# Reordering the small products of two recurrences (RWKV-7 and retention) in a hybrid decoder block

## The chip, the core and the metric

The kernel runs on one core of a Trainium2 chip. The metric is the device time of one execution in microseconds (us), the median over three executions. Comparisons of kernels are made on the same chip, beside executions of the kernel before.

## What is computed

The block takes x (1 x 1024 tokens x 1024 channels, float32) and returns the same shape. Two token mixers work side by side on the normalised tokens, a merge and an output projection follow, then a gated convolutional FFN. Only the two mixers matter here:

```python
# RWKV-7, 8 heads of 64 channels: one state S (64 x 64) per head, token by token
def step(S, inp):
    r_t, k_t, v_t, w_t, kk_t, a_t = inp
    sa = jnp.einsum('bhvk,bhk->bhv', S, -kk_t)
    S = (S * w_t[:, :, None, :]
         + sa[..., None] * (kk_t * a_t)[:, :, None, :]
         + v_t[..., None] * k_t[:, :, None, :])
    y = jnp.einsum('bhvk,bhk->bhv', S, r_t)
    return S, y
...
# retention, 8 heads (64 channels for queries and keys, 128 for values), chunks of 128 tokens
def step(R, inp):
    qc, kc, vc = inp
    s = jnp.einsum('bihd,bjhd->bhij', qc, kc) * decay_mask
    inner = jnp.einsum('bhij,bjhe->bihe', s, vc)
    cross = jnp.einsum('bihd,bhde->bihe', qc * q_decay, R)
    R = R * chunk_decay + jnp.einsum('bjhd,bjhe->bhde', kc * k_decay, vc)
    return R, inner + cross
```

## The kernel before, in words

All matrix work is done on TensorE (PE in the profile). The large projections are float32 products made exact from two parts: each of them is three products of 128 x 128 weights with 512 columns (lines L198 to L200, `mm3`). The small products of the recurrences are plain float32 products; the hardware runs each of them as two passes, so the profile counts two MATMUL records for one `PE.matmul` of the code.

The program goes in stages. First come the projections of the RWKV branch (`rw_tiles`, products `ps_rw`), with two low-rank products per channel tile and token half: `p_lw` (L400, L401) and `p_a` (L404, L405). Of each, the second part uses half of the rows only (64 of 128). Then come the two recurrences, and the other 40 projection tiles (`qk_pair`, `side_tile`, products `ps_side`) are put between their steps. Nothing in the recurrences needs most of these tiles, so they fill TensorE while the recurrence waits for other engines.

The RWKV recurrence is done in 8 blocks of 128 tokens (j), each with two chunks of 64 tokens (c). Per block and chunk:

- `p_G` (L589): products of keys with queries, 8 heads. Even heads lie on partitions 0 to 63 and odd heads on 64 to 127, so each product uses 64 rows of the array; q is the parity. The four even heads go to one PSUM bank and then the four odd heads to another one (tag "B", two banks). VectorE (DVE) evacuates each bank into `Tt` (L592) and `Gm` (L594).
- An inverse of triangular blocks: `Tt` goes through DRAM (`tt_d`, `tb`), DVE substitutes row by row (L611, L613, tiles `xprod` and `xb`), the result goes through DRAM to `XD`, is transposed by DVE to `X` (L624), and feeds products on 32 x 32 pieces of the array (L632, L639, L649, L657).
- `p_W1` (L685, L689; the profile calls the tile p_W): for each pair of heads a product of the queries with the state (128 rows, 64 columns of the array, L685) and then two head products with `Gm` (64 rows, 64 columns, L689). DVE copies the sum (L691), `p_S` follows (L695, 64 x 64), DVE makes `AV`, then `p_N` (L703, the new state; even and odd heads write different halves of the partitions), and `p_Y` (L716, L719; both 128 rows by 64 columns).

Retention is done in 8 blocks of 128 tokens. `first_stage(j)` transposes the values (`p_v`, L773), makes the masked scores `p_s` (L782, 64 rows of the array, four even heads and then four odd ones, again in two banks), and the next state `p_R` (L795). `second_stage(j)` makes the outputs `p_o` in two banks (tags "C" for even heads, "Y" for odd ones): for each head a product with the state (L818, 64 rows) and one with the scores (L819, all 128 rows), the first only for j > 0. Then come the statistics of the heads (L821), the scaling by ScalarE (ACT) from PSUM into `on` (L834), and transposes `p_y` (L840).

The order on each engine is not the order of the code. A planner with its own cost model places the instructions of all engines; the code gives dependences and buffers, and `tc.high_priority` lifts some of them. So a change in the code moves instructions that it does not name.

The core of `p_W1` and `p_o` before:

```python
for i in range(4):
    if not fresh:
        PE.matmul(p_W1[q, i * 128:(i + 1) * 128], AR[:, i, 1 + c, :], state[:, i, :],
                  start=True, stop=False)
    for h in (2 * i, 2 * i + 1):
        hs = slice(64 * h, 64 * h + 64)
        PE.matmul(p_W1[q, hs], Gm[c][o, hx(h), 64 - 64 * c:128 - 64 * c], AV[c][o, hs],
                  start=fresh, stop=fresh or h % 2 == 1)
```

Of the kernel before, what the change touches and what calls it, by code (L numbers as in the profile page):

```python
# [41 lines left out]
def constants():  # L42
# [8 lines left out]
    # columns that sum the even and the odd head of tile i: rows 2i, 2i+1 of 8 (two sums of 8 rows)  # L51
# [12 lines left out]
    # rows 8g..8g+7 of the unit matrix of 16 for the partitions of group g  # L64
# [8 lines left out]
    # decays of the queries (halved: the gate adds the factor), their squares (even heads, then odd), those of the keys  # L73
# [32 lines left out]
def layout(a):  # L106
# [12 lines left out]
    # columns of the rotated queries and keys: first halves of four heads, then their second halves  # L119
# [24 lines left out]
def body(tc, nc, xT, pos, wch, wbrw, wbret, wout, wup, wdn, w2a2, gw2, rows, vecs, consts0, consts1, out):  # L144
    V, S, G, PE = nc.vector, nc.scalar, nc.gpsimd, nc.tensor
    ctx = ExitStack()
    with ctx:
# [23 lines left out]
        def bank(name, tag="A"):  # L171
            return psB.tile([128, 512], F32, tag=tag, name=name, bufs=BANKS[tag])
# [4 lines left out]
        def load_w(src, kt, full=None, hi=None, lo=None, st=None):  # L177
            """Weights [128, kt, 128] as the exact sum of two float32r parts (in st, hi, lo if given)."""
# [33 lines left out]
        def rms_bcast(pool, ss, nt, tags="AA", mem=None, to=None):  # L212
            """ss holds partial sums of squares over channels, for nt tiles of 128 tokens; returns the
            reciprocal root mean square of each token on all partitions, in PSUM
            (or in to, by four tiles)."""
# [36 lines left out]
        with tc.tile_pool(name="x0", bufs=2, reuse_waits="tile") as xp:  # L252
            # the tokens go into the products before their norm, which scales what comes out
# [43 lines left out]
        # ---- RWKV projection with token shift, and what the recurrence needs of each channel tile:  # L297
        # decayed queries, key directions and keys, for all tokens
# [5 lines left out]
        with pctx, tc.tile_pool(name="p1", bufs=1, reuse_waits="tile", side="right") as p1:  # L304
# [12 lines left out]
            def rw_tiles(tiles, ws):  # L317
                """Column tiles of w_in with the token shift; of several, the first two go by quarters of the tokens at first."""
# [43 lines left out]
            # the inputs of the low-rank products as two parts, stacked on the partitions  # L362
# [4 lines left out]
            # the other products take the tokens with their norm  # L367
# [24 lines left out]
            for i in range(4):  # L392
# [4 lines left out]
                for hf in range(2):  # L397
# [3 lines left out]
                    PE.matmul(p_lw, wll[0:64, 0, ch], LW[0:64, h_], start=False, stop=True)  # L401
# [3 lines left out]
                    PE.matmul(p_a, wll[64:128, 1, ch], LA[64:128, h_], start=False, stop=True)  # L405
                    S.activation(ta[:, h_], p_a, AF.Tanh, bias=a0h[:, i1], scale=0.5)
                # decays: their sums from the start of each chunk
# [43 lines left out]
                for c in range(2):  # L451
                    # the chunks of a pair swapped
                    o = 2048 + 128 * i + 64 * (1 - c)
                    nc.scalar.dma_start(L_d[:, :, o:o + 64].rearrange("j p t -> p j t"), v_.rearrange(jct, c=2, t=64)[:, :, c, :])
            # the sums over each head's channels, token-major; those for the values with the chunks swapped
# [12 lines left out]
            # rotary tables, packed: sines, then cosines, each by halves of the tokens  # L468
# [21 lines left out]
        # ---- the other projections: rotated queries and keys, values, gates  # L490
        pj_d = dp.tile([40, 128, T], F32, name="pj_d")

        def qk_pair(m):
            """Tiles 14 + 2m, 15 + 2m of w_in: both halves of the queries or keys of four heads."""
# [26 lines left out]
        def side_tile(i):  # L521
            """Column tile i of w_in (22..29 v, 30..37 g, 38..53 gates)."""
# [15 lines left out]
        # ---- RWKV-7 in chunks of 64 tokens, two chunks (one tile of 128 tokens) at a time  # L538
# [24 lines left out]
        for j in range(NJ):  # L563
# [7 lines left out]
            # token-major values, chunk c in the rows of the other one  # L571
# [8 lines left out]
            # products of the keys with the queries  # L580
            Gm = []
            Tt = r2.tile([128, 8, 64], F32, name="Tt")
            for c in range(2):
                gm = r2.tile([128, 8, 128], F32, tag=f"Gm{c}", name="Gm")
                for q in range(2):
                    p_G = bank("p_G", "B")
                    lo = 64 * q
                    for i in range(4):
# [692 lines left out]
```

## Time and profile before

| what | value |
|---|---|
| runs of the kernel before | 1952.18, 1954.6 and 1958.46 us, median 1954.6 |
| span of the profiled execution | 1949.9 us, the one time of that execution that the page gives |
| PE, PEld (weight loads) | busy 95% and 75% of the span |
| DVE, ACT, POOL | busy 61%, 33% and 38% of the span |
| mean granted TensorE clock | 0.978 |
| chain of work that ended last | PE 60%, DVE 21%, DMA 7%, issue 5%, POOL 4%, ACT 3% |
| RWKV recurrence | about 240 to 746 us of the span |
| retention | about 760 to 918 us |
| last `ps_side` product, first merge product after it | 951.4 and 951.7 us |

The span runs from the first to the last instruction of one execution. A matmul's duration in the profile is a modelled latency, and matmuls are pipelined: what one costs the engine is read from its start to the start of the next one. The shape "64*128" in a row means 64 rows by 128 columns of the array. The granted clock is given as a share of full speed: 1.0 is 2.4 GHz and 0.5 is 1.2 GHz.

### The profile page before, as it was taken

The page shows a single profiled execution, that of the slowest core. Times are in us where ns is not written, and L with a number is a line of the kernel's source. Part 1 is how long each engine was busy: PE and PEld are TensorE (multiplying, and loading weights), DVE is VectorE, ACT ScalarE, POOL GpSimd, SP SyncE. Part 2 cuts the span into 40 slices and gives each one's busy share as a digit, 9 for nine tenths or more (in the row PEclk, how much of TensorE's full clock was granted, in tenths as well). Part 3 has the DMA queues.
Part 4 walks back from the last instruction along what each step waited for, and adds up shares of the span by engine and source line. Part 5 has one row for each costly group of instructions (what it writes and reads, how often), then busy time and mean ns, then how long its engine had stood idle before and what let it go on. Part 6 is the DMA issues. An engine that isn't in the chain of part 4 may idle for free.

```text
span 1949.9 us, 27421 instructions
## 1 busy us (share of the span) xinstructions
PE 1848.0 (95%) x10626; PEld 1471.4 (75%) x10626; DVE 1191.9 (61%) x2003; ACT 650.3 (33%) x999; POOL 742.9 (38%) x534
## 2 busy tenths in 40 slices
PE   6889989999999999999999999789999999999996
PEld 5667877777777778777788878567777777778885
DVE  7885474744565534564253855879988887753413
ACT  4544221111111112232244334444444444543320
POOL 4755433221221022011264753654544544322523
PEclk8899999999999999999999999899999999999998
DMA  4443532342333225444563643533222222675521
GB/s 170 135 135 119 180 92 64 109 111 86 100 99 101 68 71 173 147 140 131 204 201 104 225 145 126 184 122 108 87 76 87 67 76 74 211 216 154 184 89 43
DMA packets 203841, 244.43 MB, mean 125 GB/s; under 512 B 61120, under 2 KB 136384, under 8 KB 202688
## 3 DMA queue, kind: packets, MB, share of 16 engines
q1 hardware_dynamic: 126864, 171.11, 28.3%
q10 hardware_dynamic: 76848, 71.59, 11.3%
q8 instruction: 83, 1.36, 0.3%
q14 instruction: 46, 0.38, 0.1%
HBM read 177.10 MB, written 65.54 MB: 124 GB/s over the span
## 4 chain that ended last, share of the span: by engine, by line
PE 60%; DVE 21%; DMA 7%; issue 5%; POOL 4%; ACT 3%; ACTq 0%; SPq 0%; DVEq 0%; POOLq 0%
PE ps_side L200 7%; PE ps_side L198 7%; PE ps_side L199 7%; DVE u_f L1037 4%; PE ps_dn L200 4%; PE ps_dn L198 3%; PE ps_dn L199 3%; DVE u_f L1039 2%; POOL w_lo L1131 2%; PE ps_rw L198 2%; PE ps_rw L199 2%; PE ps_rw L200 2%; DVE w_sa L1135 2%; PE ps_o L199 1%; PE ps_o L200 1%
## 5 line engine op out<-in xcount | busy, mean ns | idle before, releaser
L192 POOL TENSOR_TENSOR w_lo<-w_st,w_hi 128x1024 fp32r<-128x1024 f32 (+2 forms) x107 | 250.7, 2344 | 508.2 <-PE ps_side L200 174.3
L187 ACT CAST w_hi<-w_st 128x1024 fp32r<-128x1024 f32 (+2 forms) x162 | 161.8, 999 | 441.8 <-PE ps_side L199 160.1
L199 PE MATMUL ps_side<-hnl,w_hi 128*128 128x512 f32 x640 | 255.8, 400 | 0.0
L200 PE MATMUL ps_side<-hnh,w_lo 128*128 128x512 f32 x640 | 255.5, 399 | 0.0
L198 PE MATMUL ps_side<-hnh,w_hi 128*128 128x512 f32 x640 | 255.3, 399 | 0.0
L192 DVE TENSOR_TENSOR w_lo<-w_st,w_hi 128x1024 fp32r<-128x1024 f32 (+1 forms) x55 | 71.8, 1306 | 139.2 <-ACT w_hi L187 42.4
L200 PEld LDWEIGHTS ps_side<-hnh,w_lo 128*128 128x128 f32 x640 | 121.0, 189 | 26.6 <-issue 0.8
L199 PEld LDWEIGHTS ps_side<-hnl,w_hi 128*128 128x128 f32 x640 | 121.1, 189 | 26.1 <-issue 1.3
L198 PEld LDWEIGHTS ps_side<-hnh,w_hi 128*128 128x128 f32 x640 | 120.9, 189 | 25.7 <-issue 0.5
L1037 DVE SCALAR_TENSOR_TENSOR u_f<-ub,vct,u_f 128x512 f32<-128x512 f32 x88 | 103.4, 1179 | 9.5 <-ACT u_f L1036 9.5
L1131 POOL TENSOR_TENSOR w_lo<-w_st,w_hi 128x512 fp32r<-128x512 f32 (+1 forms) x53 | 106.0, 2024 | 1.7 <-issue 1.6
L1036 ACT ACTIVATE u_f<-ub,vct 128x512 f32<-128x512 f32 x76 | 60.0, 813 | 123.6 <-DVE ub L1169 102.3
L199 PE MATMUL ps_rw<-hnl,w_hi 128*128 128x512 f32 (+1 forms) x224 | 89.3, 399 | 9.8 <-DVE hnl L269 8.8
L198 PE MATMUL ps_rw<-hnh,w_hi 128*128 128x512 f32 (+1 forms) x224 | 88.1, 397 | 9.1 <-ACT hnh L268 7.1
L200 PE MATMUL ps_rw<-hnh,w_lo 128*128 128x512 f32 (+1 forms) x208 | 81.0, 390 | 0.0
L200 PE MATMUL ps_b<-y_hi,w_lo 128*128 128x512 f32 x192 | 75.4, 393 | 1.9 <-POOL w_lo L192 1.0
L198 PE MATMUL ps_b<-y_hi,w_hi 128*128 128x512 f32 x192 | 75.4, 393 | 0.4 <-ACT w_hi L187 0.4
L199 PE MATMUL ps_b<-y_lo,w_hi 128*128 128x512 f32 x192 | 75.3, 392 | 0.0
L200 PE MATMUL ps_dn<-f_k,w_lo 128*128 128x512 f32 (+1 forms) x198 | 73.0, 369 | 0.0
L198 PE MATMUL ps_dn<-f_k,w_hi 128*128 128x512 f32 (+1 forms) x198 | 72.9, 368 | 0.0
L1039 DVE SCALAR_TENSOR_TENSOR u_f<-ub,vct,u_f 128x512 f32<-128x512 f32 x88 | 72.7, 843 | 0.2
L199 PE MATMUL ps_dn<-f_k,w_hi 128*128 128x512 f32 (+1 forms) x198 | 72.7, 368 | 0.0
(422 smaller groups left out, 4503.2 us busy)
## 6 DMA issues: line engine op xcount, KB each, us to landing
w_st<-in_wup_dram SPq DMA_DIRECT2D x54, 512.0 KB, 3.5
w_st<-in_wch_dram SPq DMA_DIRECT2D x52, 512.0 KB, 3.7
w_st<-in_wdn_dram SPq DMA_DIRECT2D x38, 512.0 KB, 4.0
pj_d<-ot ACTq DMA_DIRECT2D x64, 256.0 KB, 2.0
zvg<-pj_d SPq DMA_DIRECT2D x8, 1536.0 KB, 8.7
f_d<-u_f ACTq DMA_DIRECT2D x44, 256.0 KB, 2.1
L<-L_d SPq DMA_DIRECT2D x8, 1344.0 KB, 6.1
gt<-pj_d SPq DMA_DIRECT2D x32, 256.0 KB, 4.3
```

The source lines that it names most:

```text
L187: S.copy(hi, st)
L192: eng.tensor_tensor(out=lo, in0=st, in1=hi, op=ALU.subtract)
L198: PE.matmul(ps, wh, xh, start=first and a == 0, stop=False, skip_group_check=skip)
L199: PE.matmul(ps, wh, xl, start=False, stop=False, skip_group_check=skip)
L200: PE.matmul(ps, wl, xh, start=False, stop=last and a == n - 1, skip_group_check=skip)
L1036: S.activation(u, src, AF.Identity, bias=VC("cb")[:, i:i + 1], scale=VC("cw2")[:, i:i + 1])
L1037: V.scalar_tensor_tensor(out=u, in0=ub[:, 1:513], scalar=VC("cw1")[:, i:i + 1], in1=u, op0=ALU.mult, op1=ALU.add)
L1039: V.scalar_tensor_tensor(out=u, in0=ub[:, 0:512], scalar=VC("cw0")[:, i:i + 1], in1=u, op0=ALU.mult, op1=ALU.add)
L1131: eng.tensor_tensor(out=w[1][:, ks, :], in0=src, in1=w[0][:, ks, :], op=ALU.subtract)
L1135: V.tensor_tensor(out=sa[:, rh_, :], in0=st1[:, lh, :], in1=st2[:, lh, :], op=ALU.subtract)
```

## The change

Five groups of products are written in another order or another shape; the sums are the same. Comments were dropped too, which shifts nothing but line numbers (L589 becomes L590, L685 becomes L692, L689 becomes L688, L782 becomes L785, L818 becomes L820, L819 becomes L824).

```diff
                     PE.matmul(p_lw, wlh[:, 0, ch], LW[:, h_], start=True, stop=False)
-                    PE.matmul(p_lw, wll[0:64, 0, ch], LW[0:64, h_], start=False, stop=True)
+                    PE.matmul(p_lw, wll[:, 0, ch], LW[:, h_], start=False, stop=True)
...
-                    PE.matmul(p_a, wll[64:128, 1, ch], LA[64:128, h_], start=False, stop=True)
+                    PE.matmul(p_a, wll[:, 1, ch], LA[:, h_], start=False, stop=True)
...
+                p_Gs = [bank("p_G", "B") for q in range(2)]
+
+                for i in range(4):
+                    for q in range(2):
+                        lo = 64 * q
+                        PE.matmul(p_Gs[q][:, i * 128:(i + 1) * 128], BK[lo:lo + 64, i, 2 * c:2 * c + 2, :],
+                                  AR[lo:lo + 64, i, 2 * c:2 * c + 2, :], start=True, stop=True)
                 for q in range(2):
-                    p_G = bank("p_G", "B")
-                    lo = 64 * q
-                    for i in range(4):
-                        PE.matmul(p_G[:, i * 128:(i + 1) * 128], BK[lo:lo + 64, i, 2 * c:2 * c + 2, :],
-                                  AR[lo:lo + 64, i, 2 * c:2 * c + 2, :], start=True, stop=True)
...
-                for i in range(4):
-                    if not fresh:
+
+                for h in range(8):
+                    hs = slice(64 * h, 64 * h + 64)
+                    PE.matmul(p_W1[q, hs], Gm[c][o, hx(h), 64 - 64 * c:128 - 64 * c], AV[c][o, hs],
+                              start=h == 0, stop=fresh, skip_group_check=True)
+                if not fresh:
+                    for i in range(4):
                         PE.matmul(p_W1[q, i * 128:(i + 1) * 128], AR[:, i, 1 + c, :], state[:, i, :],
-                                  start=True, stop=False)
-                    for h in (2 * i, 2 * i + 1):
-                        hs = slice(64 * h, 64 * h + 64)
-                        PE.matmul(p_W1[q, hs], Gm[c][o, hx(h), 64 - 64 * c:128 - 64 * c], AV[c][o, hs],
-                                  start=fresh, stop=fresh or h % 2 == 1)
+                                  start=False, stop=True, skip_group_check=True)
...
+            p_ss = [bank("p_s", "B") for e in range(2)]
+            for i in range(4):
+                for e in range(2):
+                    lo = 64 * e
+                    PE.matmul(p_ss[e][:, i * 128:(i + 1) * 128], Z[lo:lo + 64, 4 + i, :], Z[lo:lo + 64, i, :],
+                              start=True, stop=True)
             for e in range(2):
-                p_s = bank("p_s", "B")
-                lo = 64 * e
-                for i in range(4):
-                    PE.matmul(p_s[:, i * 128:(i + 1) * 128], Z[lo:lo + 64, 4 + i, :], Z[lo:lo + 64, i, :],
-                              start=True, stop=True)
...
-            p_os = []
+            p_os = [bank("p_o", "CY"[e]) for e in range(2)]
+
+            if j:
+                for i in range(4):
+                    for e in range(2):
+                        lo = 64 * e
+                        PE.matmul(p_os[e][:, i * 128:(i + 1) * 128], Z[lo:lo + 64, i, :], Rj[lo:lo + 64, i, :],
+                                  start=i == 0, stop=False, skip_group_check=True)
             for e in range(2):
-                p_o = bank("p_o", "CY"[e])
-                p_os.append(p_o)
-                lo = 64 * e
                 for i in range(4):
-                    s_ = slice(i * 128, (i + 1) * 128)
-                    if j:
-                        PE.matmul(p_o[:, s_], Z[lo:lo + 64, i, :], Rj[lo:lo + 64, i, :], start=True, stop=False)
-                    PE.matmul(p_o[:, s_], sm[:, e * 4 + i, :], vt[:, 2 * i + e, :], start=j == 0, stop=True)
+                    PE.matmul(p_os[e][:, i * 128:(i + 1) * 128], sm[:, e * 4 + i, :], vt[:, 2 * i + e, :],
+                              start=j == 0 and i == 0, stop=True, skip_group_check=True)
```

What moves on the engines, at three places. First TensorE, block 0, second chunk of the RWKV recurrence, where `p_W1` is made (p_W_1962 is that tile; p_X and p_Y are other small products). Before, with the first two of its four pairs of groups:

```order
L639 MATMUL p_X<-XD,W 32x32 x17
L685 MATMUL p_W_1962<-state_1690,L 64x128
L689 MATMUL p_W_1962<-AV,Gm 64x64 x2
L685 MATMUL p_W_1962<-state_1690,L 64x128
L689 MATMUL p_W_1962<-AV,Gm 64x64 x2
```

Now:

```order
L722 MATMUL p_Y<-AV,Gm 64x64 x8
L641 MATMUL p_X<-XD,W 32x32 x17
L688 MATMUL p_W_1962<-AV,Gm 64x64 x8
L692 MATMUL p_W_1962<-state_1690,L 64x128 x4
L719 MATMUL p_Y<-state_1690,L 64x128
```

The eight head products stand together and the four state products stand behind them; before, the two kinds alternated four times.

Second TensorE, a late block of retention, where `p_o` is made between transposes p_y of the block before and p_k (on and sm are SBUF tiles, R the state). Before, the start of it:

```order
L840 MATMUL p_y<-cst_69,on 128x128 x4
L819 MATMUL p_o<-vt,sm 128x128
L840 MATMUL p_y<-cst_69,on 128x128 x4
L818 MATMUL p_o<-R,zvg 128x128
L819 MATMUL p_o<-vt,sm 128x128
L818 MATMUL p_o<-R,zvg 128x128
```

Now, the whole of it:

```order
L820 MATMUL p_o<-R,zvg 128x128 x4
L847 MATMUL p_y<-cst_69,on 128x128 x8
L820 MATMUL p_o<-R,zvg 128x128 x4
L824 MATMUL p_o<-vt,sm 128x128 x2
L793 MATMUL p_k<-cst_69,zvg 128x128 x4
L824 MATMUL p_o<-vt,sm 128x128 x6
```

The state products stand in two runs and the score products in two, where each product stood nearly alone before. Over all blocks the order has the 56 state products in 53 runs before and in 17 now.

Third DVE, block 0 of the RWKV recurrence, where `XD` is transposed to `X` (xprod and xb belong to the substitution of block 1). Before:

```order
L613 TENSOR_REDUCE xb<-xprod 128x8
L611 TENSOR_TENSOR xprod<-xb,tb 128x8x7
L613 TENSOR_REDUCE xb<-xprod 128x8
L624 STREAM_TRANSPOSE X<-XD 128x256
L611 TENSOR_TENSOR xprod<-xb,tb 128x8x8
```

Now:

```order
L594 TENSOR_TENSOR Tt<-p_G,rna 64x256
L596 TENSOR_TENSOR Gm<-p_G,cst_77 128x512
L626 STREAM_TRANSPOSE X<-XD 128x256
L613 TENSOR_TENSOR xprod<-xb,tb 128x8x2
L615 TENSOR_REDUCE xb<-xprod 128x8
```

The transpose stood behind six steps of the next block's substitution and now stands ahead of all of them. From the merge to the end of the program the order on all engines is the same in both, but for one weight load on SP's queue at its start.

## Rows read from the trace of the kernel before

**Rows 1.** The page, busy time of TensorE and its weight loads.
```profile
PE 1848.0 (95%) x10626; PEld 1471.4 (75%) x10626; DVE 1191.9 (61%) x2003; ACT 650.3 (33%) x999; POOL 742.9 (38%) x534
```
**Rows 2.** Busy time by stretch: PE, PEld, DVE, ACT, POOL, clock, DMA share, GB/s.
```profile
320.00:720.00 400.00, 399.43 (x3772) 312.74 (x3771) 217.51 (x614) 69.32 (x110) 78.09 (x77) 1.00 0.31 91
760.00:910.00 150.00, 150.00 (x912) 117.92 (x910) 85.23 (x281) 37.60 (x82) 16.74 (x11) 1.00 0.45 134
```
**Rows 3.** Timeline of PE: start, us, line, operation, tile, shape; one p_W1 and p_S.
```profile
713.96 0.43 PE L685 MATMUL p_W<-state,L 128*64 128x128 f32 x2
...
716.90 0.43 PE L716 MATMUL p_Y<-state,L 128*64 128x128 f32 x2
...
722.49 1.14 PE L695 MATMUL p_S<-W,XT 64*64 64x64 f32 x16
723.56 0.50 PE L200 MATMUL ps_side<-hnh,w_lo 128*128 128x512 f32 x1
```
**Rows 4.** Timeline of PE in retention: p_o, pairs of groups.
```profile
903.24 0.48 PE L818 MATMUL p_o<-R,zvg 64*128 64x128 f32 x2
903.65 0.71 PE L819 MATMUL p_o<-vt,sm 128*128 128x128 f32 x4
904.29 0.49 PE L818 MATMUL p_o<-R,zvg 64*128 64x128 f32 x2
904.71 0.49 PE L819 MATMUL p_o<-vt,sm 128*128 128x128 f32 x2
```
**Rows 5.** Timeline of PE: p_N alternates between two column halves, p_Y does not.
```profile
323.18 0.69 PE L703 MATMUL p_N<-AV,BKt 128*64 128x64 f32 x16
323.70 1.10 PE L719 MATMUL p_Y<-AV,Gm 128*64 128x64 f32 x16
324.72 0.50 PE L639 MATMUL p_X<-XD,W 32*32 32x32 f32 x34
```
**Rows 6.** Timeline of PE and PEld: p_G, both parities in one piece, then one alone.
```profile
240.88 1.71 PE L589 MATMUL p_G<-L 64*128 64x128 f32 x16
242.52 0.50 PE L198 MATMUL ps_side<-hnh,w_hi 128*128 128x512 f32 x1
...
240.88 1.52 PEld L589 LDWEIGHTS p_G<-L 64*128 64x128 f32 x16 [0.17 <-issue]
...
640.55 1.13 PE L589 MATMUL p_G<-L 64*128 64x128 f32 x8 [0.57 <-DVE Gm L594]
641.61 0.50 PE L198 MATMUL ps_side<-hnh,w_hi 128*128 128x512 f32 x1
```
**Rows 7.** Timeline of PE: one pair of low-rank products among the projections.
```profile
105.08 0.40 PE L400 MATMUL p_lw<-LW,wlh 128*128 128x512 f32 x1
105.41 0.49 PE L401 MATMUL p_lw<-LW,wll 64*128 64x512 f32 x1
105.83 0.50 PE L198 MATMUL ps_rw<-hnh,w_hi 128*128 128x512 f32 x1
106.17 0.39 PE L199 MATMUL ps_rw<-hnl,w_hi 128*128 128x512 f32 x1
106.40 0.40 PE L200 MATMUL ps_rw<-hnh,w_lo 128*128 128x512 f32 x1
```
**Rows 8.** Timeline of PE: two waits in block 0, and products after the second.
```profile
250.16 1.01 PE L589 MATMUL p_G<-L 64*128 64x128 f32 x7 [1.32 <-DVE Gm L594]
...
291.13 0.75 PE L632 MATMUL p_W<-X,Tt 32*32 32x32 f32 x64 [4.46 <-DVE X L624]
...
292.25 0.63 PE L198 MATMUL ps_side<-hnh,w_hi 128*128 128x512 f32 x1
292.67 0.63 PE L199 MATMUL ps_side<-hnl,w_hi 128*128 128x512 f32 x1
```
**Rows 9.** Timeline of ACT and PE: evacuation of p_o and the next block's first product.
```profile
855.99 2.55 ACT L834 ACTIVATE on<-p_o,nb,rh 128x128 f32<-128x128 f32 x7
...
858.55 0.49 PE L818 MATMUL p_o<-R,zvg 64*128 64x128 f32 x2
```
**Rows 10.** Groups of instructions by line: DVE's copy between p_W1 and p_S.
```profile
L691 DVE COPY W<-p_W 64x512 f32<-64x512 f32 x16 | 11.0, 688 | 33.3 <-PE p_W L689 33.2
```

More of the change, by code (lines that the diff above doesn't have):

```diff
@@ L584, in body @@
                 gm = r2.tile([128, 8, 128], F32, tag=f"Gm{c}", name="Gm")
-                for q in range(2):
-                    p_G = bank("p_G", "B")
-                    lo = 64 * q
-                    for i in range(4):
-                        PE.matmul(p_G[:, i * 128:(i + 1) * 128], BK[lo:lo + 64, i, 2 * c:2 * c + 2, :],
-                                  AR[lo:lo + 64, i, 2 * c:2 * c + 2, :], start=True, stop=True)
-                    g4 = p_G.rearrange("p (h t) -> p h t", h=4)
+                p_Gs = [bank("p_G", "B") for q in range(2)]
[4 more added lines that the diff above has]
+                                  AR[lo:lo + 64, i, 2 * c:2 * c + 2, :], start=True, stop=True)
+                for q in range(2):
+                    g4 = p_Gs[q].rearrange("p (h t) -> p h t", h=4)
                     V.tensor_tensor(out=Tt[sw[c], 4 * q:4 * q + 4, :], in0=g4[sw[c], :, sw[1 - c]],
@@ L777, in first_stage @@
             sm = t2.tile([128, 8, 128], F32, name="sm")
-            for e in range(2):
-                p_s = bank("p_s", "B")
-                lo = 64 * e
-                for i in range(4):
-                    PE.matmul(p_s[:, i * 128:(i + 1) * 128], Z[lo:lo + 64, 4 + i, :], Z[lo:lo + 64, i, :],
-                              start=True, stop=True)
-                V.tensor_tensor(out=sm[:, 4 * e:4 * e + 4, :], in0=p_s.rearrange(h4, h=4), in1=rmask, op=ALU.mult)
+            p_ss = [bank("p_s", "B") for e in range(2)]
[4 more added lines that the diff above has]
+                              start=True, stop=True)
+            for e in range(2):
+                V.tensor_tensor(out=sm[:, 4 * e:4 * e + 4, :], in0=p_ss[e].rearrange(h4, h=4), in1=rmask, op=ALU.mult)
             Rj = R
@@ L809, in second_stage @@
             mv = t2.tile([128, 8, 2], F32, name="rmv")
-            p_os = []
+            p_os = [bank("p_o", "CY"[e]) for e in range(2)]
[5 more added lines that the diff above has]
+                                  start=i == 0, stop=False, skip_group_check=True)
             for e in range(2):
-                p_o = bank("p_o", "CY"[e])
-                p_os.append(p_o)
-                lo = 64 * e
                 for i in range(4):
-                    s_ = slice(i * 128, (i + 1) * 128)
-                    if j:
-                        PE.matmul(p_o[:, s_], Z[lo:lo + 64, i, :], Rj[lo:lo + 64, i, :], start=True, stop=False)
-                    PE.matmul(p_o[:, s_], sm[:, e * 4 + i, :], vt[:, 2 * i + e, :], start=j == 0, stop=True)
+                    PE.matmul(p_os[e][:, i * 128:(i + 1) * 128], sm[:, e * 4 + i, :], vt[:, 2 * i + e, :],
+                              start=j == 0 and i == 0, stop=True, skip_group_check=True)
+            for e in range(2):
                 for i in range(4):
-                    V.bn_stats(out=st[:, 4 * e + i, :], in_=p_o[:, i * 128:(i + 1) * 128])
+                    V.bn_stats(out=st[:, 4 * e + i, :], in_=p_os[e][:, i * 128:(i + 1) * 128])
                     V.bn_aggr(out=mv[:, 4 * e + i, :], in_=st[:, 4 * e + i, :])
```

## The prediction

> **What bounds the kernel now.** I read the page first: TensorE is busy for 95% of the span [rows 1], far above any other engine. Then the stretches. In the RWKV recurrence TensorE is busy for 399.4 of 400 us and in retention for 150.0 of 150, at a granted clock of 1.00 (2.4 GHz), while DVE, the next, has 217.5 and 85.2 [rows 2]. So through both recurrences the end is set by how fast TensorE gets through its queue: the side projections fill every wait, and any time that a small product gives back lets the rest of the queue come earlier. "Busy" says nothing of how well it is used, because a record's duration is a latency. So the third view is the timeline of PE, where a cost is the distance from one start to the next.
>
> Two things are to be seen there. One is a price for changing the shape in which the array is used. In `p_o` four passes with 128 rows take 0.64 us (903.65 to 904.29) and two passes with 64 rows take 0.42 (904.29 to 904.71), as do the two before (903.24 to 903.65, 0.41) [rows 4]. Where four cost 0.64 and two 0.42, two more passes cost 0.22, or 0.11 each, and each group pays 0.20 for the change. The other is that products on different halves of the array run side by side. `p_N`, whose heads alternate between two column halves, needs 0.52 us for 16 passes; `p_Y`, the same shape on one half, needs 1.02 [rows 5]. For row halves, `p_G` gives a hint: 8 passes on one half take 1.06 us (640.55 to 641.61), 16 on both halves in one piece 1.64, less than twice 1.06 [rows 6]. The second half starts while the first is still running, but late, since its products stand behind all of the first.
>
> **The change part by part.**
>
> `p_W1`, fewer changes of shape. Before, one chunk takes 2.94 us (713.96 to 716.90): four state groups and four head groups in turn [rows 3]. Now the eight head products stand in one run; `p_S` is the same shape and number and takes 1.07 us up to the next product (722.49 to 723.56) [rows 3]. The four state products are 8 passes at 0.11, 0.88 us [rows 4], and are mostly followed by `p_Y`, of the same shape. That is 1.95, so 0.99 us less per chunk, in 15 chunks (the first has no state): **14.9 us**. Bounds: 0.79 if one more change of 0.20 is left in a chunk, 1.19 if one less; 12 to 18 us.
>
> `p_o`, fewer changes and row halves side by side. The order of the program had 53 runs of state products and has 17 now. Each run that goes saves two changes of 0.20 [rows 4]: 36 x 0.40 = 14.4 us. The 56 products themselves cost 56 x 0.22 = 12.3 us; alternated, at the ratio of 0.52 to 1.02 [rows 5], 6.3. Some runs are too short for that, so I take 5 us and not 6. Together **19.4 us**, between 14.4 (halves give nothing) and 20.4.
>
> `p_G`, row halves side by side. A set of 16 passes cost 1.64 us in one piece; if both halves run at once from the start, it costs what one half costs, 1.06 [rows 6]. 16 sets x 0.58 = **9.3 us**. The lower end is 0, if the halves overlap no more than now. The upper is 17, if every set had been in two pieces (2.12 against 1.06); in the order before, 9 of 16 sets stand in one piece, so I stay near the lower price.
>
> `p_s`, the same at 8 sets: 8 x 0.58 = **4.6 us**, between 0 and 4.6; all sets stand in one piece before and after.
>
> `p_lw` and `p_a`: the second part with all 128 rows has more multiplications but the same time, and no change of shape. The three starts around a pair are 0.33, 0.42 and 0.34 us apart, where three products in a row take 3 x 0.23 [rows 7]: 0.40 per pair, 16 pairs, 6.4 us. For the first half of the pairs TensorE later waits for other engines, so it would only wait longer; I count eight, **3.2 us**, between 0 and 6.4.
>
> The sum is 14.9 + 19.4 + 9.3 + 4.6 + 3.2 = **51.4 us**. It is taken from a span of 1949.9 us, which gives 1898.5.
>
> Waits are moved too, since the planner orders anew. In block 0 TensorE waits 4.46 us for `X`, and afterwards a product takes 0.42 us (292.25 to 292.67) where 0.23 is usual [rows 7, 8]: that is half clock, 1.2 GHz, granted after the wait. In the new order DVE transposes `X` ahead of the next block's substitution, and the load of `XD` stands ahead of that block's `tb` in SP's queue. That could give up to some 5 us back. Against it stand two new conditions. `p_G` now needs both banks of tag "B" before its second product, where the wait in block 0 was 1.32 us [rows 8]; another evacuation by DVE, about 1.1 us, lies in between. And `p_o` needs both banks from the start: the odd heads' bank is free only after the last four of eight ACT instructions, at 2.55 / 7 = 0.36 us each [rows 9] 1.5 us later than the even heads'. In the block shown the state product came 0.01 us after the last of them (855.99 + 2.55 = 858.54, then 858.55), so that place has little room. I put the gain and these losses at zero together, from -10 to +5 us. No DMA is added, and DVE, ACT and POOL get no new instruction; only their places change. After retention the order is the same as before and I expect it to take the same time, only earlier.
>
> The Trainium skill bears on the halves. Its page "TensorE: Matmul & The Clock Gate" (LDWEIGHTS) says that loading weights takes as long as their columns at 1.2 GHz, however few rows they have. By it a load of 128 columns takes an estimated 107 ns, and if the loads of both halves went one after another, 16 of them would take an estimated 1.71 us, no set of `p_G` or `p_s` could get shorter, and the sum would be 51.4 - 19 = 32. The trace speaks against it: the 16 loads of one set were over in 1.52 us.
>
> **The rivals.**
>
> First, **row halves give nothing more**. Column halves overlap [rows 5], and different row halves might share something that column halves do not. For it: in one piece the set still took 1.64, not 1.06 [rows 6]. Against it: 16 passes at 0.11 would be 1.76 and the two changes come on top, so some overlap is there already. Without p_G, p_s and 5 us of p_o the gain is 51.4 - 9.3 - 4.6 - 5 = 32.5: 1954.6 - 32.5 = 1922.
>
> Second, **the two banks make new waits**. If each of 7 blocks of `p_o` waits 1.5 us [rows 9] and 16 sets of `p_G` wait 1.1, that is 28 us, and 1954.6 - 51.4 + 28 = 1931; half of them is likelier, 1917. For it: the tight place in rows 9. Against it: side projections stand between these steps, and the planner knows of both banks. The skill's page "TensorEngine Tiling (Array Packing)" (Restrictions and Gotchas) speaks against the change in the same way: row tiles need different PSUM banks, so tiling rows raises the pressure on PSUM. The rows show one such case of tightness and no wait from it.
>
> Third, **slower: the hand-over from chunk to chunk starts to wait**. State products now stand last in `p_W1`, directly ahead of the copy and `p_S`. If TensorE, being faster, reached `p_S` or the state products too early in each of 15 chunks and waited as in block 0, 4.46 us plus some 1.6 us for products at half clock [rows 8], that is 15 x 6.1 = 91 us, and 1954.6 - 51.4 + 91 = 1994. It decides from 51.4 / 15 = 3.4 us per chunk on. Against it: between the end of `p_W1` and `p_S` lie 5.6 us of other products (716.90 to 722.49) [rows 3], and the copy needs 0.69 [rows 10]; the new order keeps about as many products there.
>
> Fourth, **nothing is gained**: the pauses at a change of shape were covered by something that stays, say the pipeline's own drain. Then it is 1954.6. The pitch of `p_Y`, whose two kinds have the same shape, speaks against it.
>
> **How the numbers follow.** The forecast has 0.68: 1954.6 - 51.4 = **1903 us** against the median of the runs (the profiled execution is 4.7 us below that median, and I carry the difference along). Row halves without gain have 0.12 (1922), new waits 0.14 (1917 to 1931), slower 0.03 (1994), nothing gained 0.03. The range for 8 in 10 goes down to 1889, where p_G's upper price (some 8 us) and the given-back wait (5) come together, and up to 1921, which takes in half of the waits and nearly the first rival. About 0.3% (6 us) is what a measurement can tell from no change. Faster by more than that: the forecast and the first two rivals, 0.94; the same 0.03; slower 0.03.
>
> **What would show it.** In the new profile one `p_W1` should take about 1.95 us in two runs, a set of `p_G` or `p_s` 1.06 to 1.2 us instead of 1.64, and `p_o` should show long runs at 0.11 (score products) and about 0.055 (state products) per pass. The first merge product should start about 50 us earlier than 951.7, with DVE's busy time unchanged and TensorE still busy all through both recurrences. If a set of `p_G` still takes 1.64, the first rival holds; if idle time with DVE or ACT as releaser shows up ahead of `p_G` or `p_o`, the second; if ahead of `p_S` or state products, at a clock below 1.00 between 320 and 700 us, the third.

## The result and the profile after

| | before | changed |
|---|---|---|
| median of the runs | 1955.3 us (4 runs, 1952.18 to 1958.46) | 1909.31 us (4 runs, 1908.35 to 1910.88) |
| ratio, 95% interval | | 0.9769 [0.9755, 0.9783] |
| span of the profiled execution | 1949.9 us | 1908.9 us |

The change takes 46 us off the median; the forecast was 51.4 less, to 1903, in a range from 1889 to 1921. Between the two profiled executions the spans differ by 41.0 us, since that of before lay 5.4 us below the median of 1955.3 and that of the changed kernel 0.4 below its own. So 10.4 us of the 51.4 are missing in the profile, and the question is which terms they belong to. One execution of one kernel below, `p_Y` on both column halves, ran at a mean granted clock of 0.654 (2515.64 us) where all others had 0.97 to 0.98; it is not in that kernel's ratio, and its trace is not read.

First the page of the changed kernel, busy time of TensorE, which answers to [rows 1].

```profile
PE 1802.9 (94%) x10626; PEld 1448.7 (76%) x10626; DVE 1180.5 (62%) x2003; ACT 648.8 (34%) x999; POOL 742.9 (39%) x534
```

PE is 45 us less busy with the same 10626 instructions. DVE is 11 us less busy, which the prediction had as unchanged; no run explains that. The view of busy time by stretch of the changed kernel (PE, PEld, DVE, ACT, POOL, clock, DMA share, GB/s), both recurrences, answers to [rows 2].

```profile
320.00:690.00 370.00, 368.70 (x3655) 294.94 (x3653) 212.73 (x607) 66.68 (x107) 77.33 (x76) 1.00 0.33 96
735.00:862.00 127.00, 125.48 (x887) 101.99 (x885) 77.29 (x268) 36.01 (x80) 14.37 (x10) 1.00 0.50 155
```

TensorE still works all the time, so it still sets the end; the gaps are 1.3 and 1.5 us. Next the timeline of PE of the changed kernel: one `p_W1`, one set of `p_G`, two blocks of `p_o` (the first two runs in block 2, the last three lines in block 7), and the start of the merge. They answer to [rows 3], [rows 6] and [rows 4].

```profile
338.11 1.14 PE L688 MATMUL p_W<-AV,Gm 64*64 64x64 f32 x16
339.18 1.09 PE L692 MATMUL p_W<-state,L 128*64 128x128 f32 x8
340.20 0.50 PE L200 MATMUL ps_side<-hnh,w_lo 128*128 128x512 f32 x1
...
239.82 1.16 PE L590 MATMUL p_G<-L 64*128 64x128 f32 x16
240.91 0.50 PE L198 MATMUL ps_side<-hnh,w_hi 128*128 128x512 f32 x1
...
769.60 1.16 PE L820 MATMUL p_o<-R,zvg 64*128 64x128 f32 x8
770.68 0.50 PE L200 MATMUL ps_side<-hnh,w_lo 128*128 128x512 f32 x1
...
771.78 1.16 PE L820 MATMUL p_o<-R,zvg 64*128 64x128 f32 x8
772.87 0.50 PE L199 MATMUL ps_side<-hnl,w_hi 128*128 128x512 f32 x1
...
859.04 1.16 PE L820 MATMUL p_o<-R,zvg 64*128 64x128 f32 x12
860.12 2.05 PE L824 MATMUL p_o<-vt,sm 128*128 128x128 f32 x16
861.93 0.48 PE L199 MATMUL ps_side<-hnl,w_hi 128*128 128x512 f32 x1
...
909.02 0.39 PE L198 MATMUL ps_b<-y_hi,w_hi 128*128 128x512 f32 x1
```

A `p_W1` takes 2.09 us here (338.11 to 340.20) where it took 2.94; over the 15 chunks with a state it takes 1.78 to 2.23, most often 2.00. A set of `p_G` takes 1.09 us where one took 1.64. In `p_o` the 16 score products in a row run at 1.81 / 16 = 0.11 us per pass. But of its state products one run of 8 passes takes 1.08 us and the next again 1.09: no halves side by side there, while 12 passes in block 7 take no more (1.08). The merge begins at 909.02 instead of 951.7, 42.7 us earlier.

To put a number on each term I added up, over all products of a line, the distance from a product's start to the next start on PE (waits that follow are in it):

| products | before | changed | gain | forecast |
|---|---|---|---|---|
| `p_W1` | 46.4 | 31.8 | 14.6 | 14.9 |
| `p_o` | 43.0 | 27.6 | 15.4 | 19.4 |
| `p_G` | 32.0 | 22.9 | 9.1 | 9.3 |
| `p_s` | 13.0 | 8.7 | 4.3 | 4.6 |
| `p_lw`, `p_a` | 15.0 | 11.2 | 3.8 | 3.2 |

Two lines hold more than the price read for one chunk or set. Of `p_W1`, 0.8 us come from the first chunk, which has no state products and so no change of shape in either kernel. The timeline of PE shows it, before and then changed:

```profile
251.31 1.97 PE L689 MATMUL p_W<-AV,Gm 64*64 64x64 f32 x16
253.20 0.79 PE L199 MATMUL ps_side<-hnl,w_hi 128*128 128x512 f32 x1
```
```profile
249.26 1.14 PE L688 MATMUL p_W<-AV,Gm 64*64 64x64 f32 x16
250.33 0.50 PE L198 MATMUL ps_side<-hnh,w_hi 128*128 128x512 f32 x1
```

The same 16 passes take 1.89 us behind the wait of 1.32 us ahead of `p_G` [rows 8], at a granted clock of 0.50, and 1.07 at 1.00. The 15 other chunks give 13.8 us, 0.92 each. And not every set of `p_G` went from 1.64 to 1.09: the mean of the 16 went from 2.00 to 1.43, since in both kernels some sets are cut by other products or hold a wait.

The last line deceives. The views of PE's waits from 60 to 224 us, first before, then changed (total us, times, longest):

```profile
PE p_a L404 <- DVE LA L385: 6.8, 1, 6.8
PE p_a L404 <- ACT ta L406: 3.8, 1, 3.8
PE ps_rw L198 <- DVE v__786 L341: 1.8, 1, 1.8
```
```profile
PE p_a L404 <- DVE LA L385: 6.8, 1, 6.8
PE ps_rw L198 <- DVE v__786 L341: 3.4, 1, 3.4
PE p_a L404 <- ACT ta L406: 2.2, 1, 2.2
PE p_lw L400 <- ACT th L402: 1.1, 1, 1.1
PE p_sb L449 <- ACT rk_h L351: 1.0, 1, 1.0
```

With the smaller ones the waits are 13.8 us before and 17.4 now, 3.6 more. Some of them lie inside the distances of the last line of the table, 0.3 us before and 2.0 now. Without them the products give 5.4 us back (14.7 less 9.2, rounded), and the projection product behind each pair 0.9 more in all, so together about the 6.4 of all 16 pairs; the waits took most of it again. The first `ps_side` starts at 222.45 instead of 223.86 and the first `p_G` at 239.82 instead of 240.88, so 1.1 to 1.4 us are left of this term.

And PE's waits from the first `p_G` to the merge, before and then changed:

```profile
PE p_W L632 <- DVE X L624: 4.5, 1, 4.5
PE p_G L589 <- DVE Gm L594: 1.9, 2, 1.3
```
```profile
PE p_W L634 <- DVE X L626: 2.4, 3, 1.1
PE p_X L641 <- DVE W L635: 2.4, 1, 2.4
PE p_v L776 <- DMA zvg<-pj_d: 1.5, 3, 1.0
PE p_v L574 <- ACT AV L578: 0.7, 1, 0.7
PE p_G L590 <- DVE Gm L596: 0.2, 1, 0.2
```

The wait for `X` in block 0 did shrink, but `p_X` behind it waits 2.4 us instead, and new ones came up. In all TensorE is idle for 6.4 us of this stretch before and 7.3 now (the rows are rounded).

### The profile page after: what moved, and what is told of

Read it like the earlier page. It is cut to its first block, busy times and chain, and to the rows that moved or that the text cites. A ratio compares the mean times of both kernels' runs of the same rounds, so it can differ in the third digit from the quotient of the medians.

```text
span 1908.9 us, 27427 instructions
## 1 busy us (share of the span) xinstructions
PE 1802.9 (94%) x10626; PEld 1448.7 (76%) x10626; DVE 1180.5 (62%) x2003; ACT 648.8 (34%) x999; POOL 742.9 (39%) x534
## 4 chain that ended last, share of the span: by engine, by line
PE 48%; DVE 18%; DMA 9%; issue 4%; POOL 3%; ACT 3%; ACTq 0%; SPq 0%; DVEq 0%; POOLq 0%
PE ps_side L199 6%; PE ps_side L200 6%; PE ps_side L198 6%; DVE u_f L1044 4%; PE ps_dn L200 3%; PE ps_dn L199 3%; PE ps_dn L198 3%; POOL w_lo L1138 2%; DVE u_f L1046 2%; DMA w_st<-in_wup_dram 2%; DVE w_sa L1142 2%; PE ps_o L199 2%; PE ps_o L200 1%; PE ps_o L198 1%; DVE w_sa L1141 1%
## 5 line engine op out<-in xcount | busy, mean ns | idle before, releaser
L192 DVE TENSOR_TENSOR w_lo<-w_st,w_hi 128x1024 fp32r<-128x1024 f32 (+1 forms) x55 | 75.2, 1368 | 130.0 <-ACT w_hi L187 41.3
```

The costliest lines, as they stand in the source:

```text
L192: eng.tensor_tensor(out=lo, in0=st, in1=hi, op=ALU.subtract)
```

## The experiments

All are compared with the kernel before, run on the same chip; "us less" is 1 minus the ratio, times 1954.6.

**The four parts alone**, each in the kernel before, to see whether the terms are worth what the table says and whether they add up.

Only `p_W1`:

```diff
-                for i in range(4):
-                    if not fresh:
-                        PE.matmul(p_W1[q, i * 128:(i + 1) * 128], AR[:, i, 1 + c, :], state[:, i, :],
...
+                for h in range(8):
...
+                if not fresh:
+                    for i in range(4):
```

> The kernel before with the new p_W1 alone: eight head products in one run, then the four state products. Theory: TensorE sets the end and the price is that of the changes of shape, so what the products give back comes out whole: p_W1 costs 46.4 us in all before and 31.8 in the changed kernel (start to start), so 14.6 us less, about 1940. Rival (the order around it, not the changes of shape): p_W1 in one run leaves less for TensorE to do between the copy and p_S, new waits take a third or more back, and the gain is under 10 us. Rival (the parts disturb one another in the changed kernel): alone it gives more than 14.6, up to the 18 of the upper bound.

Only `p_o`:

```diff
-                p_o = bank("p_o", "CY"[e])
...
+            p_os = [bank("p_o", "CY"[e]) for e in range(2)]
...
+                for i in range(4):
+                    for e in range(2):
```

> The kernel before with the new p_o alone. Theory: fewer changes of shape and, where even and odd heads alternate in the planner's order, row halves side by side. In this kernel's order every block but the first has 2 state products of even heads, 2 of odd heads and then 4 that alternate, so some more overlap than in the changed kernel, where p_o went from 43.0 to 27.6 us: 15 to 18 us less, about 1938. Rival (no overlap of halves, changes of shape alone): 36 runs less at 0.40 is 14.4. Rival (both banks from the start make a new wait of 1.5 us in each of 7 blocks): 15 - 10 = 5 us less, about 1950.

Only `p_G` and `p_s`:

```diff
-                for q in range(2):
-                    p_G = bank("p_G", "B")
-                    for i in range(4):
+                p_Gs = [bank("p_G", "B") for q in range(2)]
+                for i in range(4):
+                    for q in range(2):
```

> The kernel before with the new p_G and p_s alone: even and odd heads alternate, both banks taken before the first product. Theory: row halves side by side, a set 1.10 us instead of 1.64: 9.1 us from p_G and 4.3 from p_s, 13.4 us less, about 1941. Rival (halves give nothing, the gain in the changed kernel came from sets that the planner no longer cuts in two): sets of 16 passes keep about 1.64 and the gain is under 5 us. Rival (new waits for two banks at tag B): the sets get shorter and the time falls by under 7 us, with idle time before p_G released by DVE.

Only the low-rank products:

```diff
-                    PE.matmul(p_lw, wll[0:64, 0, ch], LW[0:64, h_], start=False, stop=True)
+                    PE.matmul(p_lw, wll[:, 0, ch], LW[:, h_], start=False, stop=True)
```

> The kernel before with the second parts of p_lw and p_a over all 128 rows alone. Theory: two changes of shape less for each pair, 3.6 us by start to start over 16 pairs, but TensorE waits for DVE and ACT in this stage, and the first ps_side comes only about 1.4 us earlier: 0 to 2 us less, within the noise. Rival (as the prediction had it: half of the pairs count): 3.2 us less. Rival (all count): 6.4 us less.

| part | ratio, interval | us less | products, start to start |
|---|---|---|---|
| `p_W1` | 0.9938 [0.9924, 0.9951] | 12.1 | 13.4 less |
| `p_o` | 0.9933 [0.9917, 0.9949] | 13.1 | 16.1 less |
| `p_G`, `p_s` | 0.9923 [0.9908, 0.9938] | 15.1 | 14.9 less |
| `p_lw`, `p_a` | 0.9995 [0.9985, 1.0005] | 1.0 | 3.6 less |

The sum is 41.3 us, beside 45.2 for all four (0.9769), a difference that lies within the intervals: no disturbance of one part by another shows, and each of the first three gives nearly what its products give back. The low-rank part gives nothing that can be told from zero, as its waits say. `p_o` alone loses 3 us; the view of PE's waits of that run, from the first `p_G` to the merge, shows to what:

```profile
PE p_v L773 <- DMA zvg<-pj_d: 4.8, 6, 1.1
```

With shorter blocks of retention the next block's operands land too late, six times.

**Halves in turn again.** Is it the alternation, or only that both banks are taken first?

```diff
-                for i in range(4):
-                    for q in range(2):
+                for q in range(2):
+                    for i in range(4):
```

(and the same in `p_s`).

> The changed kernel, but p_G and p_s go first through the even heads and then through the odd ones again; both banks are still taken before the first product. Theory: it is the alternation that lets row halves run side by side, so a set goes back to about 1.64 us and 22.9 + 8.7 us of p_G and p_s become about 45: 13 us more than the changed kernel, ratio to before about 0.983. Rival: taking both banks first, so that the planner puts a set in one piece, was what helped; then a set stays near 1.1 and the ratio near the changed kernel's 0.977.

Ratio 0.9858 [0.9842, 0.9873], 1924.39 us, 15 us more than the changed kernel (17 by the two ratios). The timeline of PE shows the set of `p_G` that took 1.09 us:

```profile
239.78 1.71 PE L590 MATMUL p_G<-L 64*128 64x128 f32 x16
241.41 0.50 PE L198 MATMUL ps_side<-hnh,w_hi 128*128 128x512 f32 x1
```

That is 1.63 us, as before the change. `p_G` and `p_s` cost 43.2 us instead of 31.6; the rest is mostly 1.9 us more idle time of TensorE (9.3 instead of 7.3) and more projection products at half clock (20 instead of 7, some 2.5 us). So the order even, odd, even, odd is what shortens a set, and the first rival falls.

**`p_W1` in two groups**, to price a change of shape by its dose.

```diff
-                for h in range(8):
+                for g in range(2):
+                    for h in range(4 * g, 4 * g + 4):
...
-                    for i in range(4):
+                        for i in (2 * g, 2 * g + 1):
```

> The changed kernel, but p_W1 in two groups (four head products, two state products, and again). Theory: each two changes of shape more cost the same; from four groups to one gave 14.6 us in 15 chunks, so one group more costs a third, 4.9 us: 0.32 us more in a chunk, ratio to before about 0.9795. Rival: the gain came from the place of the state products (last, beside p_Y) and not from the number of changes; then nearly all of the 14.6 is kept or nearly all is lost.

Ratio 0.991 [0.9895, 0.9926], 1935.02 us: 26 us more than the changed kernel, not 5. The price itself is as expected. In the timeline of PE of this run, the second chunk of block 2 (the first group of head products takes 0.60, 438.08 to 438.68):

```profile
438.92 0.65 PE L692 MATMUL p_W<-state,L 128*64 128x128 f32 x4
439.50 0.68 PE L688 MATMUL p_W<-AV,Gm 64*64 64x64 f32 x8
440.11 0.65 PE L692 MATMUL p_W<-state,L 128*64 128x128 f32 x4
440.59 0.38 PE L719 MATMUL p_Y<-state,L 128*64 128x128 f32 x2
```

0.60 + 0.58 + 0.61 + 0.48 = 2.27 us, 0.27 to 0.28 more than the commonest chunk of the changed kernel (2.00); over the 13 chunks of this run that hold no wait and no half clock the mean is 0.31 more. In 15 chunks that is some 4 us. The rest came with the order that the planner made for this kernel. From the first `p_G` to the last `ps_side` TensorE is idle for 14.8 us instead of 7.3, and the mean granted clock of that stretch is 0.98 instead of 1.00. Two of the places, in the same view:

```profile
429.28 1.08 PE L634 MATMUL p_W<-X,Tt 32*32 32x32 f32 x64 [3.68 <-DVE X L626]
...
430.88 0.63 PE L198 MATMUL ps_side<-hnh,w_hi 128*128 128x512 f32 x1
431.31 0.63 PE L199 MATMUL ps_side<-hnl,w_hi 128*128 128x512 f32 x1
...
617.18 0.44 PE L688 MATMUL p_W<-AV,Gm 64*64 64x64 f32 x4
619.31 1.58 PE L742 MATMUL p_g<-wg,L 128*128 128x512 f32 x2 [1.69 <-DVE xb L615]
620.82 0.69 PE L688 MATMUL p_W<-AV,Gm 64*64 64x64 f32 x4
```

A wait for `X` of block 3, where the changed kernel waits at most 1.1 us for an `X`, and `p_g` put into the middle of a `p_W1`, waiting for DVE. After each, products come at 0.43 us and not 0.23, the clock of 1.2 GHz. So neither theory as I wrote it holds for the time: the dose is right for the products, and the new order cost some 21 us besides.

**ScalarE takes the heads of `p_o` in turn.** Why do the halves of `p_o` seldom run side by side? ScalarE empties the even heads' bank first, and the planner then puts even state products where the odd heads' bank is still full.

```diff
-            for e in range(2):
-                for i in range(4):
+            for i in range(4):
+                for e in range(2):
                     q = 4 * e + i
                     S.activation(on[:, q, :], p_os[e][:, i * 128:(i + 1) * 128], AF.Identity,
```

> The changed kernel, but ScalarE scales the heads of p_o from its two banks in turn (even, odd, even, odd) instead of all even heads first; nothing else is touched. Both banks then come free together. Theory: p_o fell short of its term because the even heads' bank comes free some 1.5 us earlier and the planner puts all even state products first, so that in several blocks no halves run side by side (runs of 8 passes 1.09 us, one parity). In this kernel's order the parities alternate in all 7 blocks, so the state products go from 13.8 us to about 7 x 2 x 0.64 = 9 us: 4 to 5 us less than the changed kernel, ratio to before about 0.9745. Rival: halves of p_o do not overlap for another reason, or the state products now wait for both banks: no change, 0.977.

Ratio 0.9759 [0.9743, 0.9775], 1904.59 us. The state products fell from 13.8 to 10.7 us (expected: about 9), the score products rose from 13.8 to 14.4, so `p_o` in all went from 27.6 to 25.0. By the ratios to before, this is only 2 us less than the changed kernel, by the medians 4.7. So it was run again, beside the changed kernel on one chip:

> The changed kernel itself, once more, beside the next three on the same chip. Both theories: 0.977 to before; it is the measure for the next three.

> The kernel in which ScalarE takes the heads of p_o from its banks in turn, once more, beside the changed kernel. Theory (halves of p_o now run side by side in every block; its state products cost 10.7 us instead of 13.8 in the first profile): 3 to 5 us less than the changed kernel. Rival (the first difference lay within the noise of two chips): the same within 2 us.

The changed kernel: 0.9778 [0.976, 0.9797], 1909.38 us (1907.68 to 1913.81); this one 0.975 [0.9734, 0.9766], 1903.66 us (1903.29 to 1906.74). Over both tries no run of the one reaches into the range of the other; on the one chip it is 5.7 us less. The timeline of PE of the second try, one block:

```profile
789.75 0.71 PE L820 MATMUL p_o<-R,zvg 64*128 64x128 f32 x8
790.40 1.09 PE L847 MATMUL p_y<-cst,on 128*128 128x128 f32 x8
791.42 0.71 PE L820 MATMUL p_o<-R,zvg 64*128 64x128 f32 x8
792.06 0.71 PE L824 MATMUL p_o<-vt,sm 128*128 128x128 f32 x4
```

Now 8 passes take 0.65 us where one parity alone took 1.08: 0.20 for the change and 0.055 per pass, the numbers of the forecast. One half at a time, the 17 runs and 112 passes of state products would take an estimated 17 x 0.20 + 112 x 0.11 = 15.7 us; against that the halves give 1.9 us in the changed kernel and 5.0 here, the 5 of the forecast. This shows that the halves' missing part was the order, and that the order of the evacuation sets it. Of the 5.7 us less, `p_o` accounts for 2.5; where the others come from is not shown. The two spans of this second try differ by 8.7 us, and 4.8 of them lie behind the last `ps_side`, in steps that the edit does not touch.

**`p_Y` on both column halves.** The head products of the two chunks write different column halves and could run side by side as `p_N` does.

```diff
-                    for h in (2 * i, 2 * i + 1):
-                        hs = slice(64 * h, 64 * h + 64)
-                        PE.matmul(p_Y[q, hs], Gm[c][:, hx(h), 64 * c:64 * c + 64], AV[c][:, hs],
...
+            for h in range(8):
+                hs = slice(64 * h, 64 * h + 64)
+                for c in range(2):
+                    PE.matmul(p_Y[64 * c:64 * c + 64, hs], Gm[c][:, hx(h), 64 * c:64 * c + 64], AV[c][:, hs],
```

> The changed kernel, but the head products of p_Y (whose output columns are the upper half of the array for one chunk and the lower for the other) are kept back until both chunks of a block are there, and then alternate between the two column halves; the state products of p_Y stand alone in runs of four. Theory: as with p_N, 0.52 us for 16 passes, the 32 passes of a block take about 1.05 us instead of 2.1; p_Y goes from 30.9 us to 22 to 23: 8 us less, ratio to before about 0.973. Rival: nothing fills TensorE at the end of a block, the second chunk's products come later and the group norm with them, and what is saved turns into waits: 0.977 or more.

1909.25 us, ratio 0.9782 [0.9767, 0.9798]: nothing gained. Why is not shown for this kernel, whose trace is not read. With the evacuation in turn as well:

> The kernel with the heads of p_o evacuated in turn, and p_Y's head products of both chunks alternating between the two column halves. Theory: p_Y 22 to 23 us instead of 30.9, and TensorE sets the end, so 8 us less than the kernel with the evacuation alone, about 1897. Rival, after the earlier run that gained nothing from p_Y alone: p_Y does get shorter, but what it gives back turns into waits or half clock within the recurrence; then no less than the evacuation alone, and the trace shows more idle time of TensorE or more products at half clock between the first p_G and the last ps_side than the 7.3 us of idle time in the changed kernel.

1901.45 us (1900.34 to 1908.18), ratio 0.9742 [0.9722, 0.9762]: the lowest median of all, but not to be told from the evacuation alone. The timeline of PE of that run:

```profile
441.94 1.10 PE L723 MATMUL p_Y<-AV,Gm 128*64 128x64 f32 x30
442.97 0.75 PE L641 MATMUL p_X<-XD,W 32*32 32x32 f32 x64
```

30 passes take 1.03 us, where 16 took 1.02 [rows 5]. `p_Y` went from 31.0 to 23.2 us, as expected. But the state products of `p_W1` and `p_N`, which had stood beside `p_Y` in the same shape, cost 1.4 and 0.8 us more, and `p_G` and `p_g` 1.6; from the first `p_G` to the last `ps_side` 4.7 us are left. The rival I wrote, waits, is not it: idle time is 7.1 us, beside 6.4 with the evacuation alone.

**State products first in `p_W1`**: as few changes of shape, in the other order.

```diff
+                if not fresh:
+                    for i in range(4):
...
                 for h in range(8):
...
-                if not fresh:
-                    for i in range(4):
```

> The changed kernel, but in p_W1 the four state products come first and the eight head products behind them: as few changes of shape, but the state, which comes last of all operands, is needed before 1.07 us of head products instead of behind them. Theory A (the number of changes of shape is all that counts, TensorE's queue sets the end): a p_W1 stays at about 2.0 us and the time at the changed kernel's, within 3 us. Theory B (after the run with two groups, which lost 26 us and not 5: an order in which p_W1 waits for the state, or in which the planner moves other steps late, brings waits and half clock): 10 to 25 us more, with waits ahead of the state products or of X and a granted clock below 1.00 within the recurrence.

1920.67 us, ratio 0.9837 [0.9813, 0.9861]: 11 us more than the changed kernel beside it. `p_W1` costs 33.3 us, 1.5 more; no wait stands ahead of the state products. The largest waits of PE from 237 to 920 us are elsewhere:

```profile
PE p_v L775 <- DMA zvg<-pj_d: 5.6, 4, 2.0
PE p_X L641 <- DVE W L635: 2.4, 1, 2.4
PE p_yT L745 <- DVE yn L742: 2.0, 2, 1.6
```

TensorE is idle for 13.6 us there instead of 7.5 in the changed kernel beside it. So theory B is right in its size and in that the planner moves other steps late, wrong in that `p_W1` waits for the state. What makes the planner choose so was not tried.

## Why the prediction was right, and where its sum was off

The frame held: TensorE sets the end in both recurrences, so most of what its products give back arrives, and the forecast of 1903 is 6 us from 1909.3. That the terms of the table come so near owes something to luck, as the first two points say.

- `p_W1`: 14.6 for 14.9, of which 0.8 is the clock in the first chunk and no change of shape; the 15 chunks of the term gave 13.8, 0.92 each for 0.99. The price of a change of shape, read from start to start, was nearly right, and the run with two groups confirms it by dose (0.28 to 0.31 us for one group more in a chunk, forecast 0.99 / 3 = 0.33). The run with the state products first, as few changes in the other order, costs 1.5 us more and not 14.
- `p_G`, `p_s`: 9.1 and 4.3 for 9.3 and 4.6. The price of a set in one piece, 1.64 to 1.09, was right; that `p_G` in all came to its term, though its mean set went from 2.00 to 1.43, was luck in part. The page "TensorE: Matmul & The Clock Gate" (LDWEIGHTS) of the Trainium skill gives an estimated 107 ns for a load of 128 columns; taken one after another, 16 of them would be 1.71 us. The trace does not agree with loads one after another, since a set takes 1.09 us. The first rival fell with it.
- `p_o`: 15.4 for 19.4, **the step that failed most**. "I take 5 us" for halves side by side assumed that the order in the code is the order on the engine. By the estimate above the halves gave 1.9 us of the 5, and the changes of shape the other 13.5 of the 14.4. In three of the seven blocks of the changed kernel (2, 3 and 6) the planner put the even state products ahead of the odd ones, as the rows at 769.60 and 771.78 show; in three more (4, 5 and 7) the halves alternate in part. I had seen the cause, the odd heads' bank that comes free 1.5 us later [rows 9], but had priced it as a wait and not as an order. The buffer numbers in the order of the instructions tell the parities apart, and I had read the runs without them.
- `p_lw`, `p_a`: 3.2 forecast, 1.0 to 1.4 measured. The products gave about their 6.4 us, but waits and what else moved in that stage took back most of it and not half.
- Waits at zero net: from 6.4 to 7.3 us in the recurrences, and 2.1 us lost in all with what `p_S` and other products took more. From the merge to the end it took 1.7 us more (999.9 for 998.2), which I had put at nothing. No change is needed for that: the second profile of the same changed kernel takes 1003.0 us there, so one execution differs from the next by more than 1.7.

So 4.0 of `p_o`, 0.8 of `p_W1`, `p_G` and `p_s` together, 1.8 of the low-rank term (3.2 less 1.4), 2.1 and 1.7 make up the 10.4 us that are missing in the profile. The second rival was nearly absent as a wait for banks (0.2 us ahead of `p_G`). The Trainium skill's "TensorEngine Tiling (Array Packing)" (Restrictions and Gotchas) has row tiles raise the pressure on PSUM; here that pressure showed as an order, and the evacuation in turn, which frees both banks together, gave 2.5 us of `p_o` back, in a kernel that is 5.7 us faster. The third rival did not occur: no wait stands ahead of `p_S` or the state products in the changed kernel. When `p_W1` was written in two groups, its price came in another place: waits of 1.7 and 3.7 us, then half clock, but ahead of `p_g` and of products with `X`, not at the hand-over, and that kernel was still faster than the one before.

## What to carry to other kernels

Read what a small product costs from start to start, and look for two things in it: the price of a change of shape of the array (here 0.14 to 0.20 us each) and halves of the array that lie idle; where TensorE sets the end, both come back almost whole. Where a planner sets the order, code that alternates is not yet an order that alternates: look which buffer comes free first, and make those that are to run together come free together. And when one edit is judged by its time alone, keep in mind that a new order can cost 10 to 20 us by itself, so read the products' own cost beside it.

## What the runs showed of the hardware

- Row halves run fully side by side where the queue alternates between them, and only in part where it does not: 16 passes of 64 rows and 128 columns take 1.09 us alternated, 1.63 us half by half, and 8 on one half 1.08 us. Column halves do the same: 30 alternated passes of `p_Y` 1.03 us, 16 on one half 1.02.
- The same wait in two executions of the same kernel was followed by 1.2 GHz in one and not in the other. In block 0 the changed kernel waits 2.36 us ahead of `p_X` in the first profile and 2.37 us in the second. Busy time by stretch from 290 to 295 us, right behind the wait, first profile and then second (the clock is the third figure from the end):

```profile
290.00:295.00 5.00, 4.75 (x75) 3.85 (x76) 4.52 (x16) 0.59 (x1) 1.19 (x1) 0.66 0.36 89
```
```profile
290.00:295.00 5.00, 5.00 (x83) 4.23 (x84) 4.45 (x17) 0.59 (x1) 1.08 (x1) 1.00 0.33 81
```

In the first the granted clock is 0.66 in this stretch and the projections come at 0.43 us; in the second it is 1.00 and they come at 0.23. It costs some 1.4 us here; the 7 projection products at half clock that are named above for the changed kernel are these.
